# Encoder block on one core: every operation of the MLP in a fixed order per engine, by half products

## The chip, the cores and the metric

The kernel runs on one core of a Trainium2 chip. The metric is the device time of one execution in microseconds (us). The core's engines each work through their own instruction stream in order: TensorE (PE; its weight loads are listed as PEld), VectorE (DVE), ScalarE (ACT), GpSimd (POOL), and SyncE (SP), whose queue issues the large transfers. An instruction waits for work of other engines by semaphores. TensorE's results land in PSUM, which has eight banks of 128x512 float32 here; VectorE and ScalarE read them from there. All other tiles lie in SBUF.

## The reference

One layer: a mixer (2-D neighbourhood attention beside a gated linear attention), then an MLP, then a last norm. All is float32, 1024 tokens by 1024 columns, 4096 columns inside the MLP.

```python
def sqrelu_mlp(h, ln_g, w1, w2):
    u = rmsnorm(h, ln_g) @ w1
    return jnp.square(jax.nn.relu(u)) @ w2

def reference(...):
    h = x
    h = h + hybrid_mixer(h, ...)                # projections, two attentions, @ w_out
    h = h + sqrelu_mlp(h, ln_ff_g, w_ff1, w_ff2)
    return rmsnorm(h, ln_final_g)
```

## The kernel before

Everything is kept transposed: 128 columns on the partitions, 512 tokens (`H`) or all 1024 along the free dimension. A float32 product is made of three TensorE products with a reduced-precision type: each operand x is split into a high part (`h`, a cast on ScalarE) and a low part (`l = x - h`, a difference on VectorE or GpSimd, in `to_two`), and h·h, h·l and l·h are added in PSUM. So each 128x512 operand costs one cast and one difference, and each 128x128 by 128x512 block costs three matmuls.

The projections, the two attentions and `w_out` come first; they are the same program before and after. The residual sum lies in `hT`, the normalized MLP input of the first 512 tokens in `n0`. Then comes the MLP, in eight chunks of 512 of the 4096 inner columns. Chunk 0 is computed plainly (`FirstPlain` for w1, `SecondPlain` for w2, 16 half products each). Meanwhile the second 512 tokens are normalized (`normed_h`, from the factor `r1`), and the sums of the MLP input that the later chunks need are formed (`sums123`, `sum4`, helped by `whole`, which adds a high and a low part on GpSimd).

Chunks 1 to 7 use Winograd's form of Strassen's scheme: 2x2 blocks with seven products in place of eight, in `First` (w1) and `Second` (w2). The weight quarters A11 to A22 (512 KB each, four buffers, so that a new quarter's transfer waits until an older one has been read for the last time) are combined into S1 to S4, the inner activations B11 to B22 into T1 to T4. `KW` and `KB` say which pair makes which product 1 to 7. Each product is done as two half products of 12 matmuls (128x512). In `First` a half product g gives a bank of PSUM; ScalarE copies it (line 1028) or VectorE adds it to an earlier one (1031), and the squared ReLU is taken by ScalarE (1025, 1026) or in one VectorE instruction (1032). In `Second` a product's two halves i = 0, 1 accumulate in the same four banks j = 0 to 3, and after i = 1 VectorE adds the banks to `hT` (1078).

What sets the order: TensorE's matmuls, the transfers and ScalarE's casts keep the order in which the code issues them. `go_on` calls `prep_to`, which prepares two half products ahead (the sums that they need, casts and differences), then `mm` issues the 12 matmuls. All other VectorE and GpSimd operations are placed by the framework's scheduler by its own priorities. The sums S and T are all on GpSimd (959, 1047 to 1054; S as one 128x1024 operation), and of each pair of `Second`'s activation halves one difference `ul` is on GpSimd and one on VectorE (894).

After the last product but one, `square` and `finish` compute the final norm: squares on ScalarE, their sum over the columns on VectorE, one matmul with ones (`vf`), the factor `fy`, the products with `hT`, and the transfers out. The last product of the last chunk is done in two halves of 256 tokens, the first with its `square` and `finish` ahead of the second.

Of the kernel before, what the change touches and what calls it, by code (L numbers as in the profile page):

```python
# [63 lines left out]
def block_kernel(ctx, tc, xT, g_mix, w_in, w_z, rpb, na_mask, gu, gb, g_gla, sel_f, sel_b,  # L64
# [42 lines left out]
    class Ordered:  # L107


        def matmul(self, *args, **kw):  # L110
            tc.keep_in_program_order(nc.tensor.matmul(*args, **kw))  # L111
# [823 lines left out]

    yg_pool.close()
# [6 lines left out]
    KB = {1: "B11", 2: "B21", 3: "B22", 4: "T4", 5: "T1", 6: "T2", 7: "T3"}  # L943
    nchunk = FF // P // FCH
    HP = H

    class Quarters:


        def __init__(self, src, order=("A11", "A21", "A22", "A12")):  # L950
            self.t = {}
            for q in order:
                self.t[q] = mw.tile([P, D], F32, tag="raw", name=q, bufs=4)
                tc.keep_in_program_order(DMA.dma_start(self.t[q], src[("A11", "A12", "A21", "A22").index(q)]))

        def sum(self, dst, a, b, op, own=False):
            t = self.t
            o = mu.tile([P, D], F32, tag="S", name=dst) if own else t[own_of[dst]]
            G.tensor_tensor(o, t[a], t[b], op=op)  # L959
            t[dst] = o  # L960

        def need(self, key):
            if key in self.t:
                return
            if key == "S1":
                self.sum("S1", "A21", "A22", ALU.add, own=True)
            elif key in ("S2", "S3"):
                self.sum("S3", "A11", "A21", ALU.subtract)
                self.sum("S2", "A22", "S3", ALU.subtract)
            elif key == "S4":  # L970
                self.sum("S4", "A12", "S2", ALU.subtract, own=True)

        def parts(self, key, i):
            self.need(key)
            ph = mp.tile([P, HP], F32R, tag="ph", name="ph", bufs=3)
            pl = mp.tile([P, HP], F32R, tag="pl", name="pl", bufs=3)
            to_two(ph, pl, self.t[key][:, i * HP:(i + 1) * HP], kept=True)
            return ph, pl

    own_of = {"S3": "A21", "S2": "A11"}  # L980
# [4 lines left out]
    def uparts(x, eng):  # L985
        uh = mp.tile([P, H], F32R, tag="uh", name="uh", bufs=3)
        ul = mp.tile([P, H], F32R, tag="ul", name="ul", bufs=3)
        to_two(uh, ul, x, eng, kept=True)
        return uh, ul

    npt = {"B11": (n0, 0), "B21": (n0, 4)}
    first, last = lambda p: p in (1, 2, 5), lambda p: p in (4, 3, 2)

    class First:

        order = [(p, g) for p in (1, 5, 6, 3, 7, 2, 4) for g in range(2)]

        def __init__(self, c):
            self.w, self.u, self.b = Quarters(w1[c]), {}, {}
            self.sums = {}  # L1000

        def prep(self, p, i):
            r = self.w.parts(KW[p], i)
            if i:
                self.w.need({1: "S1", 5: "S2"}.get(p, KW[p]))
            return r

        def mm(self, p, g, w):
            if first(p):
                self.b[p in (1, 6, 7, 4), g] = bank("mm" if p == 1 else "s", f"u{p}_{g}")  # L1010
            o = self.b[p in (1, 6, 7, 4), g]
            t, k0 = npt[KB[p]]
            for k in range(4):
                for a, x in ((w[0], 0), (w[0], 1), (w[1], 0)):
                    PE.matmul(o, a[:, k * P:(k + 1) * P], t[:, k0 + k, x, :], start=first(p) and k == x == 0 and a is w[0],
                              stop=k == 3 and a is w[1], skip_group_check=True)
            self.evac(p, g, o)

        def evac(self, p, g, o):
            u = self.u  # L1020
            if p in (1, 5, 6, 4):
                k = {1: "B11", 5: "B22", 6: "B12", 4: "B21"}[p]
                u[k, g] = ub(f"u{k}{g}")
                if p == 4:
                    S.activation(u[k, g], o, AF.Relu)
                    S.activation(u[k, g], u[k, g], AF.Square)
                else:
                    S.copy(u[k, g], o)
            else:
                t = u[{2: "B11", 7: "B22", 3: "B12"}[p], g]  # L1030
                V.tensor_tensor(t, t, o, op=ALU.add)
                V.scalar_tensor_tensor(t, t, 0.0, t, op0=ALU.max, op1=ALU.mult)

    class Second:

        order = [(p, i) for p in (1, 5, 6, 3, 7, 2, 4) for i in range(2)]

        def __init__(self, c, u):
            self.w, self.u, self.b, self.c = Quarters(w2[c]), u, {}, c

        def prep(self, p, i):
            u, key = self.u, KB[p]
            if (key, i) not in u:
                b11, b12, b21, b22 = (u[k, i] for k in ("B11", "B12", "B21", "B22"))
                if key == "T1":
                    u[key, i] = ub("T1")
                    G.tensor_tensor(u[key, i], b12, b11, op=ALU.subtract)  # L1047
# [9 lines left out]
            if i:  # L1057
                self.w.need({1: "S1", 5: "S2"}.get(p, KW[p]))
# [291 lines left out]
```

## Time and profile before

| | us |
|---|---|
| median of 3 runs (lowest, highest) | 1307.57 (1305.16, 1313.53) |
| profiled execution, its time | 1304.25 |
| its span, first to last instruction | 1302.5 |
| TensorE busy in it | 1182.5 |
| VectorE busy | 959.1 |
| ScalarE busy | 597.9 |
| GpSimd busy | 494.5 |
| mean granted TensorE clock | 0.955 of full |

The span runs from the first to the last instruction; the execution's own time is 1.75 us longer. The MLP takes the part from 550 us to the end. A line of the timeline gives start, duration, engine, source line, operation, output and inputs, shapes, count, and in brackets the idle time before it with what ended it. Neighbouring instructions of a kind are merged (x2, x3). The matmul of 128x512 is listed at 0.39 us, but the next one starts 0.23 us after it; the start-to-start distance is what counts.

### The profile page before, as it was taken

The numbers are of one execution on the slowest core, as the hardware profiler recorded it, in microseconds if no ns is written. First come the engines' busy times: TensorE is split into PE (matmuls) and PEld (weight loads), VectorE is DVE, ScalarE is ACT, GpSimd is POOL, SyncE is SP. The second block draws the span as 40 slices with busy tenths as digits, with TensorE's granted clock in tenths as the row PEclk, the third lists the DMA queues.
The fourth block names the chain that finished last, engine by engine and source line by source line (L and its number), as shares of the span: only waits on it lengthen the run. The fifth ranks groups of instructions, "written<-read, shape, count | busy, mean of one in ns | idle before, by whom it ended". The sixth has DMA issues, their size and how long they took to land.

```text
span 1302.5 us, 15274 instructions
## 1 busy us (share of the span) xinstructions
PE 1182.5 (91%) x5530; PEld 956.4 (73%) x5530; DVE 959.1 (74%) x1500; ACT 597.9 (46%) x1129; POOL 494.5 (38%) x290
## 2 busy tenths in 40 slices
PE   9989999899999998967899898998989989989882
PEld 8867777678778787756678686786877868868661
DVE  8787877678687865757656867957669578686796
ACT  6667547456566654344323333333333333333373
POOL 4311011222313234314533637526456175362723
PEclk8999999899999999989899999998999999999895
DMA  7211000011111422201001110110111101111003
GB/s 218 71 51 35 30 33 33 18 53 45 34 45 41 166 77 85 97 1 65 33 33 65 49 49 33 65 65 33 50 49 65 49 33 51 63 49 49 32 1 129
DMA packets 37259, 73.01 MB, mean 56 GB/s; under 512 B 8928, under 2 KB 20320, under 8 KB 37184
## 3 DMA queue, kind: packets, MB, share of 16 engines
q1 hardware_dynamic: 36608, 71.11, 16.3%
q8 instruction: 43, 0.70, 0.2%
q0 software_dynamic: 432, 0.93, 0.2%
q14 instruction: 32, 0.26, 0.1%
q10 hardware_dynamic: 144, 0.00, 0.0%
HBM read 67.84 MB, written 5.96 MB: 57 GB/s over the span
## 4 chain that ended last, share of the span: by engine, by line
PE 53%; DVE 23%; POOL 12%; ACT 6%; issue 4%; DMA 1%; SPq 0%; DVEq 0%; POOLq 0%; ACTq 0%
PE u L111 18%; PE f L111 12%; PE proj L111 11%; PE op L111 6%; DVE pl L894 3%; POOL ul L894 2%; POOL uB L1051 2%; POOL T L1047 2%; POOL A L959 2%; PE sc L111 2%; POOL S L959 2%; DVE ul L894 1%; PE no L111 1%; POOL uB L1048 1%; DVE st L567 1%
## 5 line engine op out<-in xcount | busy, mean ns | idle before, releaser
L111 PE MATMUL f<-ul,ph 128*128 128x512 f32 (+1 forms) x464 | 191.2, 412 | 37.8 <-POOL ul L894 36.5
L172 POOL TENSOR_TENSOR wl<-wf,wh 128x1024 fp32r<-128x1024 f32 x36 | 89.4, 2484 | 334.1 <-ACT wh L171 314.1
L894 DVE TENSOR_TENSOR pl<-A,ph 128x512 fp32r<-128x512 f32 x164 | 167.0, 1028 | 59.8 <-ACT ph L891 58.9
L111 PE MATMUL f<-uh,ph 128*128 128x512 f32 (+1 forms) x464 | 188.9, 407 | 6.5 <-ACT uh L891 4.6
L111 PE MATMUL f<-uh,pl 128*128 128x512 f32 (+1 forms) x464 | 187.8, 405 | 0.2 <-DVE pl L894 0.2
L891 ACT CAST ph<-A 128x512 fp32r<-128x512 f32 x164 | 101.2, 620 | 183.1 <-PE f L111 92.9
L111 PE MATMUL proj<-nh,wh 128*128 128x512 f32 x352 | 150.8, 428 | 0.2 <-DVE qd L253 0.2
L111 PEld LDWEIGHTS f<-ul,ph 128*128 128x128 f32 x464 | 93.3, 201 | 65.7 <-POOL ul L894 43.3
L959 POOL TENSOR_TENSOR S<-A,A 128x1024 f32<-128x1024 f32 x28 | 70.7, 2527 | 181.6 <-DMA A<-in_w 166.3
L111 PE MATMUL proj<-nh,wl 128*128 128x512 f32 x352 | 139.6, 397 | 0.0
L111 PE MATMUL proj<-nl,wh 128*128 128x512 f32 x352 | 139.3, 396 | 0.0
L1078 DVE TENSOR_TENSOR hT<-hT,f 128x512 f32<-128x512 f32 (+1 forms) x200 | 122.3, 664 | 0.8 <-PE f L111 0.8
L111 PEld LDWEIGHTS f<-uh,ph 128*128 128x128 f32 x464 | 93.0, 200 | 29.9 <-ACT uh L891 7.8
L111 PEld LDWEIGHTS f<-uh,pl 128*128 128x128 f32 x464 | 93.3, 201 | 18.7 <-DVE pl L894 0.4
L111 PE MATMUL u<-n,ph 128*128 128x512 f32 x288 | 90.7, 397 | 13.1 <-ACT ph L891 13.1
L894 POOL TENSOR_TENSOR ul<-uB,uh 128x512 fp32r<-128x512 f32 x42 | 62.1, 1479 | 79.5 <-ACT uh L891 74.0
L959 POOL TENSOR_TENSOR A<-A,A 128x1024 f32<-128x1024 f32 x28 | 75.4, 2693 | 38.6 <-DVE pl L894 37.6
L894 DVE TENSOR_TENSOR pl<-S,ph 128x512 fp32r<-128x512 f32 x56 | 46.6, 841 | 54.8 <-ACT ph L891 54.3
L111 PEld LDWEIGHTS proj<-nh,wh 128*128 128x128 f32 x352 | 67.0, 190 | 19.2 <-issue 5.2
L111 PE MATMUL u<-T,ph 128*128 128x512 f32 x256 | 79.9, 394 | 0.8 <-ACT ph L891 0.8
L111 PEld LDWEIGHTS proj<-nh,wl 128*128 128x128 f32 x352 | 67.1, 191 | 15.2
L111 PE MATMUL op<-y,wh 128*128 128x512 f32 x240 | 77.0, 402 | 0.4 <-DVE y L663 0.4
(297 smaller groups left out, 2601.9 us busy)
## 6 DMA issues: line engine op xcount, KB each, us to landing
A<-in_w SPq DMA_DIRECT2D x64, 512.0 KB
wf<-in_w_in SPq DMA_DIRECT2D x22, 512.0 KB
wf<-in_w_out SPq DMA_DIRECT2D x17, 512.0 KB
hT<-in_xT SPq DMA_DIRECT2D x2, 2048.0 KB
xs<-in_xT SPq DMA_DIRECT2D x6, 512.0 KB
out<-hT SPq DMA_DIRECT2D x4, 512.0 KB
out<-hT SPq DMA_DIRECT2D x8, 256.0 KB
rpb<-rpb SPq DMA_DIRECT2D x16, 96.0 KB
```

The lines of the kernel that those rows point to most:

```text
L111: tc.keep_in_program_order(nc.tensor.matmul(*args, **kw))
L172: (eng or V).tensor_tensor(wl[:, c], wf[:, c], wh[:, c].bitcast(F32), op=ALU.subtract)
L567: V.scalar_tensor_tensor(st[64:128, j - 1, :], st[64:128, j, :], dec[64:128, j:j + 1], st[64:128, j - 1, :], op0=ALU.mult, op1=ALU.add)
L891: c = S.copy(h, x)
L894: (eng or V).tensor_tensor(l, x, h.bitcast(F32), op=ALU.subtract)
L959: G.tensor_tensor(o, t[a], t[b], op=op)
L1047: G.tensor_tensor(u[key, i], b12, b11, op=ALU.subtract)
L1048: G.tensor_tensor(b12, b22, b12, op=ALU.subtract)
L1051: G.tensor_tensor(b11, b11, u["T3", i], op=ALU.add)
L1078: V.tensor_tensor(hT[:, d, c], hT[:, d, c], o[:, s], op=ALU.add)
```

## The change

Only the MLP and the last norm are written anew. Now every operation of the MLP, on every engine, keeps the order in which the code issues it (`kp`), except for a few at the start and the last norm. The same matmuls are done, except for the order of products in `First` (1, 2, 6, 5, 3, 7, 4 in place of 1, 5, 6, 3, 7, 2, 4) and of the three matmuls per block in the second products (the one with `ul` is last, it was second).

- `prepare(k)` issues what is due while half product k runs: sums from PSUM of half k-1, early sums, differences for k+1 and k+2 and casts for k+2, late sums, and the activations of half k-1.
- All S and T sums move to VectorE, each as two 128x512 operations (`Weights.sum`, `tsum`). T1, T2, T3, T4 are formed by another chain of differences; T1 is formed within `First`, and S1 and S3 of the w2 weights too (`First.late`, p = 7 and 4).
- The squared ReLU is always two ScalarE operations (`relu2`); VectorE's is gone.
- In `Second` both activation differences `ul` of a pair are on GpSimd. They wait for a gate: the last matmul of bank j = 0 of an i = 1 half, the one after which VectorE adds bank 0 to `hT`. So they run while VectorE adds from PSUM. In `SecondPlain` both are on VectorE. GpSimd keeps `whole` (now 12 calls) and a part of the last products with `fy`.
- The sum matmul for `r1` comes after one half product (it was two), and the eight normalizations of the second token half are spread over half products 2 to 7, the sums over 8 to 23.
- At the end the last product's two token halves follow each other on TensorE with only the sum for tokens 512 to 1023 (`vf_10147`) between them; the other two sums come after. The factor `gfin` is applied in the same VectorE instruction as `fy`.

```diff
-        def sum(self, dst, a, b, op, own=False):
-            o = mu.tile([P, D], F32, tag="S", name=dst) if own else t[own_of[dst]]
-            G.tensor_tensor(o, t[a], t[b], op=op)
+        def sum(self, dst, i):
+            t, (place, a, b, op) = self.t, self.table[dst]
...
+            c = slice(i * H, (i + 1) * H)
+            kp(V.tensor_tensor(t[dst][:, c], t[a][:, c], t[b][:, c], op=op))
+    def relu2(u, x):
+        kp(S.activation(u, x, AF.Relu))
+        kp(S.activation(u, u, AF.Square))
...
+    class First(Stage):
+        def late(self, p, g):
+            for key in {1: ("S2",) if g else ("S3",), 2: ("S1",)}.get(p, ()):
...
+            if p == 6:
+                self.w.sum("S4", g)
+            if p == 7:
+                t = u["B12", g]
+                kp(V.tensor_tensor(t, t, u["B11", g], op=ALU.subtract))
+            if p == 4:
+                for i in range(2):
+                    self.after.w.sum("S3" if g else "S1", i)
...
+    class Second(Stage):
+        place = {"T1": "B12", "T2": "B12", "T3": "B11", "T4": "B21"}
+        def early(self, p, i):
+            for key, n in {(1, 0): (("S2", 0),), (1, 1): (("S4", 0),), (5, 0): (("T2", 0),),
...
+                (self.w.sum if key[0] == "S" else self.tsum)(key, n)
+        def prep2(self, p, i):
+            x = self.u[self.place.get(KB[p], KB[p]), i]
+            if i:
+                self.hu[p, i] = uhigh(x)
+                self.hw[p, i] = self.w.high(KW[p], i)
+            else:
+                self.pw[p, i] = self.w.low(self.w.high(KW[p], i))
+                self.hu[p, i] = uhigh(x)
+        def prep1(self, p, i):
+            if i:
+                self.pw[p, i] = self.w.low(self.hw[p, i])
+        def lows(self, p, i, gate=None):
+            self.pu[p, i], op = ulow(self.hu[p, i], G)
+            if gate is not None:
+                tc.add_manual_dep(op.ins, gate.ins.name,
...
-                for n, (a, x) in enumerate(((wh, uh), (wh, ul), (wl, uh))):
+                for n, (a, x) in enumerate(((wh, uh), (wl, uh), (wh, ul))):
...
                 if i:
-                    self.evac(p, j, o, s)
+                    self.add(p, j, o, s)
+                if j == 0:
+                    for st, q in lows:
+                        st.lows(*q, gate=m)
...
-    def prep_to(n):
-        while len(ready) < min(n, len(halves)):
-            st, p, i = halves[len(ready)]
-            ready.append(st.prep(p, i))
+    def prepare(k):
+        halves[k - 1][0].sums(*halves[k - 1][1:])
+        st.early(p, i)
+        for n, what in ((k + 1, "prep1"), (k + 2, "prep2")):
+                getattr(halves[n][0], what)(*halves[n][1:])
+        st.late(p, i)
+        halves[k - 1][0].acts(*halves[k - 1][1:])
+        for do, args in jobs.get(k, ()):
+            do(*args)
...
+    for n, k in enumerate((2, 3, 3, 4, 5, 5, 6, 7)):
+        job(k, normed, ("B12", "B22")[n // 4], n % 4)
...
-    for c0 in (0, Q):
-        for i in range(2):
-            f2.mm(4, i, ready[k + i], slice(c0, c0 + Q))
-        for d in range(NK):
-            square(c0, Q, d)
-        finish(c0, Q, (V, V, G, V))
+    for n in range(2):
+        for i in range(2):
+            f2.mm(4, i, s=s)
+        square(n * Q, Q, range(4, 8), n)
+        if n == 0:
+            finish(H, H, sumsq(H, H, fc["h1"]), 4)
+    for n in range(2):
+        finish(n * Q, Q, sumsq(n * Q, Q, fc["h0"][:, s], fc[n]), 2)
```

How the instructions stand at three places follows. A row gives the line, the operation, the output and its inputs. First GpSimd at the start of `Second` of chunk 7, before: S sums (`A`, `S`), T sums (`T`, `uB`) and the differences `ul`.

```order
L959 TENSOR_TENSOR A_9447<-A_9445,A_9447 128x1024
L894 TENSOR_TENSOR ul<-uB_9470,uh 128x512
L959 TENSOR_TENSOR A_9445<-A_9449,A_9447 128x1024
L1047 TENSOR_TENSOR T_9727<-uB_9549,uB_9470 128x512
L1048 TENSOR_TENSOR uB_9549<-uB_9510,uB_9549 128x512
L1051 TENSOR_TENSOR uB_9470<-uB_9470,uB_9549 128x512
L894 TENSOR_TENSOR ul<-T_9727,uh 128x512
```

And the same place on GpSimd after the change:

```order
L958 TENSOR_TENSOR ul<-uB_9524,uh 128x512
L958 TENSOR_TENSOR ul<-uB_9544,uh 128x512
L958 TENSOR_TENSOR ul<-uB_9605,uh 128x512
L958 TENSOR_TENSOR ul<-uB_9623,uh 128x512
L958 TENSOR_TENSOR ul<-uB_9605,uh 128x512
```

GpSimd has nothing left there but the differences of products 1, 5, 6 and so on, two for each product. Next VectorE at the same place, before; `pl` is the low part of a weight half, `hT<-hT,f` the add of a bank to `hT`:

```order
L894 TENSOR_TENSOR pl<-A_9445,ph 128x512
L894 TENSOR_TENSOR ul<-uB_9491,uh 128x512
L894 TENSOR_TENSOR pl<-S_9710,ph 128x512 x2
L1078 TENSOR_TENSOR hT<-hT,f_0_9738 128x512
L894 TENSOR_TENSOR ul<-T_9754,uh 128x512
L1078 TENSOR_TENSOR hT<-hT,f_1_9742 128x512
```

After the change, the last VectorE rows of `First` (S1 and S3 of the w2 weights) and the first of `Second`, up to the adds of product 1 and the T2 sum of product 5:

```order
L975 TENSOR_TENSOR S_9741<-A_9492,A_9494 128x512 x2
L975 TENSOR_TENSOR A_9492<-A_9490,A_9492 128x512 x2
L975 TENSOR_TENSOR A_9490<-A_9494,A_9492 128x512
L958 TENSOR_TENSOR pl<-A_9490,ph 128x512
L958 TENSOR_TENSOR pl<-S_9741,ph 128x512
L975 TENSOR_TENSOR A_9490<-A_9494,A_9492 128x512
L975 TENSOR_TENSOR S_9741<-A_9496,A_9490 128x512
L1140 TENSOR_TENSOR hT<-hT,f_0_9796 128x512
L1140 TENSOR_TENSOR hT<-hT,f_1_9800 128x512
L1140 TENSOR_TENSOR hT<-hT,f_2_9804 128x512
L1140 TENSOR_TENSOR hT<-hT,f_3_9808 128x512
L1087 TENSOR_TENSOR uB_9605<-uB_9642,uB_9605 128x512
```

The S and T sums stand between VectorE's differences and adds now, as single 128x512 operations, and no `ul` is left there. Last, VectorE in the closing norm, before, from the factor of tokens 512 to 1023 (`fu` to `fy`, 128x512) on:

```order
L206 SCALAR_TENSOR_TENSOR fy<-ft,fy 128x512
L1078 TENSOR_TENSOR hT<-hT,f_2_9746 128x256
L1249 TENSOR_TENSOR hT<-hT,fy 128x512 x2
L1078 TENSOR_TENSOR hT<-hT,f_3_9750 128x256
L1238 TENSOR_TENSOR fsq<-fsq 128x256 x7
L201 TENSOR_SCALAR fu<-vf_10130 128x256
```

And after:

```order
L208 SCALAR_TENSOR_TENSOR fy<-ft,fy 128x512
L203 TENSOR_SCALAR fu<-vf_10213 128x256
L1360 SCALAR_TENSOR_TENSOR hT<-hT,gfin,fy 128x512 x4
L1140 TENSOR_TENSOR hT<-hT,f_0_9796 128x256
L1140 TENSOR_TENSOR hT<-hT,f_1_9800 128x256
L1140 TENSOR_TENSOR hT<-hT,f_2_9804 128x256
L1140 TENSOR_TENSOR hT<-hT,f_3_9808 128x256
L1342 TENSOR_TENSOR fsq<-fsq 128x256 x3
```

Now four products with `fy` and the first factor of tokens 0 to 255 (`vf_10213`) stand ahead of the adds of the last 256 tokens, and three sums of squares follow in place of seven.

More of the change, by code (lines that the diff above doesn't have):

```diff
@@ L991, in block_kernel, with early, late, prep1 @@
+    def relu2(u, x):
+        kp(S.activation(u, x, AF.Relu))
+        kp(S.activation(u, u, AF.Square))
     npt = {"B11": (n0, 0), "B21": (n0, 4)}
[L992 to L1011 removed]
+    class Stage:
+        gated = False
+        def early(self, p, i): pass
+        def late(self, p, i): pass
+        def prep1(self, p, i): pass
+        def sums(self, p, i): pass
+        def acts(self, p, i): pass
+        def lows(self, p, i): pass
```

373 lines of the change are left out of this document (214 added, 159 removed).

## The prediction

> **What bounds the kernel now.** I read the page's busy times first, then the chain that ended last in order of time, then the timeline of TensorE. The page:
>
> ```profile
> PE 1182.5 (91%) x5530; PEld 956.4 (73%) x5530; DVE 959.1 (74%) x1500; ACT 597.9 (46%) x1129; POOL 494.5 (38%) x290
> ```
>
> TensorE is the busiest engine; what it does not do is wait. The change keeps its work, so it can win only TensorE's waits. The chain says where the stages begin (start, duration, engine, tile, line):
>
> ```profile
> 573.92 18.24 PE u L111 x72
> 673.08 29.93 PE u L111 x132
> 1180.16 29.97 PE u L111 x132
> ```
>
> `First` of chunk 1 starts at 673.08 and of chunk 7 at 1180.16, so a chunk takes (1180.16 − 673.08) / 6 = 84.51 us. The timeline of TensorE in one of these chunks:
>
> ```profile
> 842.56 0.39 PE L111 MATMUL u<-n,pl 128*128 128x512 f32 x1
> ...
> 879.96 0.39 PE L111 MATMUL u<-T,pl 128*128 128x512 f32 x1
> ...
> 885.40 0.39 PE L111 MATMUL f<-uh,pl 128*128 128x512 f32 x1
> 886.30 0.51 PE L111 MATMUL f<-uh,ph 128*128 128x512 f32 x1 [0.51 <-ACT uh L891]
> 889.89 0.79 PE L111 MATMUL f<-ul,ph 128*128 128x512 f32 x1 [3.08 <-POOL ul L894]
> 890.48 0.63 PE L111 MATMUL f<-uh,pl 128*128 128x512 f32 x1
> ...
> 894.32 0.63 PE L111 MATMUL f<-uh,pl 128*128 128x512 f32 x1
> ...
> 898.78 0.50 PE L111 MATMUL f<-ul,ph 128*128 128x512 f32 x1 [0.81 <-POOL ul L894]
> ```
>
> From the third matmul of `First` (842.56) to its last, the 168th (879.96), are 165 steps: 37.40 / 165 = 0.2267 us. `First` never waits. A chunk's 336 matmuls at that rate are 76.17 us, so 84.51 − 76.17 = 8.34 us per chunk are lost, all in `Second`: 3.1 us on `ul` from GpSimd, 1.3 in the two short waits, and then a slow run: from 890.48 to 894.32 are nine steps of 0.427 us. The windows show the granted clock (column behind the five busy times) for it and for full work:
>
> ```profile
> 890.00:894.70 4.70, 4.70 (x11) 3.69 (x12) 2.83 (x4) 1.80 (x4) 4.62 (x3) 0.50 0.00 0
> 900.00:910.00 10.00, 10.00 (x45) 8.27 (x45) 9.68 (x16) 3.89 (x7) 1.73 (x2) 1.00 0.07 20
> ```
>
> Twelve matmuls at half clock cost 12 × (0.427 − 0.227) = 2.4 us. And the chain names what TensorE waited for, a row of GpSimd work:
>
> ```profile
> 881.00 2.90 POOL A L959
> 883.90 1.70 POOL T L1047
> 885.67 1.27 POOL uB L1048
> 887.02 1.59 POOL uB L1051
> 888.61 1.23 POOL ul L894
> ```
>
> **The chunks, part by part.** The S and T sums leave GpSimd, so 7.4 of the 8.7 us of this row go. They become VectorE work; what a difference costs there, and GpSimd's `ul`, shows in the group by tile (nanoseconds: least, median, most):
>
> ```profile
> L894 POOL TENSOR_TENSOR ul<-uB,uh x42: 1280/1462/1779, 709.0 to 1261.6; 128x512 fp32r<-128x512 f32 x42
> L894 DVE TENSOR_TENSOR ul<-uB,uh x42: 676/687/2883, 711.9 to 1264.0; 128x512 fp32r<-128x512 f32 x42
> L1078 DVE TENSOR_TENSOR hT<-hT,f x200: 405/673/682, 718.3 to 1287.7; 128x512 f32<-128x512 f32 x96, 128x256 f32<-128x256 f32 x4
> 1254.30 2.47 DVE L1078 TENSOR_TENSOR hT<-hT,f 128x512 f32<-128x512 f32 x4
> 1254.45 1.30 POOL L1054 TENSOR_TENSOR uB<-uB,uB 128x512 f32<-128x512 f32 x1 [1.83 <-DVE ul L894]
> ```
>
> A difference of two SBUF tiles takes 0.69 us alone and up to 2.88 beside GpSimd. The add from PSUM never takes over 0.68, and at 1254 four of them ran beside a GpSimd sum, 2.47 us together, both unhindered. So the gate does what it is for, if it opens in time.
>
> VectorE in `Second` after the change: 14 `pl`, four S halves, six T halves, that is 24 × 0.69 = 16.6 us, and 28 adds, 7 × 2.47 = 17.3: 33.9 us against 14 × 12 × 0.2267 = 38.1 of TensorE. In `First`: 14 `pl`, 12 S halves, two T1, six sums from PSUM, 34 × 0.69 = 23.5 against 38.1. Squared ReLU moves six VectorE operations to twelve on ScalarE, which at the page's 46% has room. So VectorE fits, but tightly: a pair of halves in `Second` lasts 5.44 us, and the common load of four adds and four differences takes 5.23; the first pair has five differences. The closest deadline is `pl` of an i = 1 half, made in the half before: VectorE ends its adds some 0.9 us into that half (the last bank closes with the previous half; then latency and one add), does one sum and this `pl` by 2.3, and TensorE wants it as its second matmul at 2.72 + 0.23 = 2.95. That is 0.65 us of slack.
>
> The new wait: `ul` at its gate. Behind it in GpSimd's queue stands only the next `ul`; TensorE waits for both. Bank 0 closes 0.68 us into the half, with a latency of 0.4 the gate is open at 1.1, the first `ul` is done at 2.4, wanted as third matmul at 3.17; the second at 3.7, wanted at 5.9. Each has about 0.8 us or more to spare. Weights: S1 and S3 now need their quarters earlier.
>
> ```profile
> 654.41 3.39 DMA A<-in_w
> ```
>
> That is how long the chain waited for a quarter. A21 and A22 for `First` are issued some 1.5 us into the last half product but one, so they should land at 4.9; the S3 sum reads A21 at about 7. Nothing is due for that. I leave 1.0 us per chunk for short waits (bounds 0 and 4, the latter half of today's loss); such waits are too short to halve the clock. Today's loss from 673.08 to the last 512-wide matmul (58 us: six chunks at 8.34, and 7.7 in the seventh, below) becomes 7: **51 us won**.
>
> At the clock a rule is worth weighing. The Trainium skill (TensorE: Matmul & The Clock Gate, Part 1, "What's actually happening") says that TensorE falls to half clock after an idle window of about 3.4 us and comes back after about as much work. The half-clock stretch above, 4.7 us behind a 3.1 us wait, agrees roughly. By it the small leftover waits of chunk 0 (below) would cost no clock either, and the sum would come out 2 us lower.
>
> **Chunk 0.** TensorE and VectorE at its start:
>
> ```profile
> 550.36 0.73 PE L111 MATMUL u<-n,ph 128*128 128x512 f32 x2 [2.01 <-ACT ph L891]
> 561.68 2.08 DVE L886 SCALAR_TENSOR_TENSOR nf<-hT,gff,r 128x512 f32<-128x512 f32 x3
> 573.92 1.22 PE L111 MATMUL u<-n,ph 128*128 128x512 f32 x2 [11.11 <-ACT ph L891]
> ```
>
> Its 384 matmuls (87.0 us) and the sum for `r1` (0.5) take 122.7 us, from 550.36 to 673.08: 35.2 lost, 11.1 of them at 573.92, where the next weight's cast stood behind all eight normalizations. Now these are spread. `r1` comes one half product earlier, 2.7 us, near 559. A cast on ScalarE, from the groups by line (count, busy us, mean ns):
>
> ```profile
> L891 ACT CAST ph<-A 128x512 fp32r<-128x512 f32 x132 | 82.0, 622 | 171.6 <-PE f L111 88.4 <-PE u L111 83.1
> ```
>
> So each normalization now costs VectorE 0.69, a wait for its cast of 0.62, and 0.69 again: 2.0 us. Eight of them and six `pl` take 16 + 4 = 20 us, up to 579; TensorE wants the last of them at the end of half product 9, at 550.4 + 1 + 27 = 578. So a wait of 1 to 3 us is left there. In the next eight halves, a pair has eight VectorE operations, two waits for casts and a GpSimd `whole` beside them, 6.2 to 7.5 us against 5.44: 3 to 8 us behind, less the lead of some 4. With one spell of half clock the loss is 2 to 15 us; I take 7, nearer the low end since the later `SecondPlain` halves are light. **28 us won** (35.2 − 7).
>
> **The end.** TensorE and VectorE in the last stretch:
>
> ```profile
> 1258.21 0.39 PE L111 MATMUL f<-uh,pl 128*128 128x512 f32 x1
> 1268.70 8.80 POOL L1249 TENSOR_TENSOR hT<-hT,fy 128x512 f32<-128x512 f32 x6 [5.82 <-DVE fy L206]
> 1268.88 3.31 DVE L1249 TENSOR_TENSOR hT<-hT,fy 128x512 f32<-128x512 f32 x2
> 1272.44 6.94 DVE L1238 TENSOR_TENSOR fsq<-fsq 128x256 f32<-128x256 f32 x7
> 1279.43 1.22 PE L111 MATMUL vf<-fsq,ones 128*128 128x256 f32 x2 [11.55 <-DVE fsq L1238]
> 1294.95 3.15 DVE L1249 TENSOR_TENSOR hT<-hT,fy 128x256 f32<-128x256 f32 x6
> ```
>
> From the last 512-wide product (T = 1258.6) to the end (1302.5) are 43.9 us, 11.6 of them TensorE waiting in `vf` for VectorE's sums. After, that sum no longer stands between the token halves, so they end near T + 10. Then VectorE is the bound, in the order shown: the factor for tokens 512 to 1023 near T + 13, four products at 3.31 / 2 each beside GpSimd (T + 20), adds of the last 256 tokens and three sums (3 us), factor and six products (4), the last factor and six products (5), and what follows the last product today, 1302.5 − 1298.1 = 4.4: T + 36. If GpSimd hinders less, T + 28; if the pile of sums ahead is later, T + 41. I take 34.5: **9.4 us won**.
>
> **Sum.** 28.2 + 50.8 + 9.4 = 88.4. Against the profiled execution's own 1304.25 that is 1215.9. The median shown is 3.3 above this execution; I put 1217.
>
> **Rivals.**
> 1. The second `ul` spills over the adds. Two `ul` take 2 × 1.28 = 2.56 us against 2.47 of adds, so it ends just after them, beside VectorE's next sum. If that sum then stands still for a whole `ul`, a pair takes 5.23 + 1.28 = 6.5 against 5.44, and 49 pairs lose 1.1 each: 1217 + 52 − 7 = 1262. Against it: the spill is 0.1 to 0.5 us, and as matmul and adds wait for the same event a late TensorE brings them into step. Chance 0.10. The Trainium skill (SBUF — State Buffer, "Who interferes with whom") has this as a rule: an operation of VectorE with two SBUF inputs and a GpSimd one that reads SBUF lock each other out for the whole instruction, and one SBUF input is free of it. The adds at 1254 agree.
> 2. VectorE is tight without that: missed deadlines of half a us in most pairs, or quarters that land late: 3 to 5 us per chunk, 1240. Chance 0.15.
> 3. Slower: GpSimd and VectorE lose step for good. Both `ul` then fall beside differences: a pair is 5.23 + 2.56 = 7.8 us, a wait of 2.4 us each, with half clock behind it another 2.4, 49 pairs: 1217 + 235 − 7 = 1445. It starts where VectorE is over 0.65 us late in each pair and TensorE's wait does not let it catch up. That the gate hangs on the same matmul as the adds speaks against it. Chance 0.04.
> 4. No change: the clock gives way when the gaps go. At a mean of 0.87 the seven chunks' 533 us of matmuls take 533 / 0.87 = 613, and 1217 + 80 = 1297. The full clock through 900 to 910, with no gap, speaks against it. Chance 0.03.
>
> **How the numbers follow.** The forecast has 0.68. Its bounds: chunk 0 at 2, no loss in the chunks and the end at T + 28 give 1217 − 5 − 7 − 6.5 = 1198; 15, 4 per chunk and T + 41 give 1253. All ends at once are unlikely; with rival 2 inside and a step toward rival 1 the range is 1199 to 1255. A gain or loss of 1%, 13 us, is what a measurement here can tell from none. Faster takes all but rivals 3 and 4: 0.93; within 1% 0.03; slower 0.04.
>
> **What would show it.** Right: `Second` as even as `First`, a chunk near 77 us, GpSimd's `ul` at 1.28 us inside the adds, no half clock after 600 us, chunk 1 starting near 645, the 11.6 us wait in `vf` gone. Wrong: `pl` or `ul` named as what TensorE waits for in every pair (rivals 1 to 3), VectorE's sums over 1 us, a clock under 0.95 without gaps, or a chunk 0 that ends after 655.

## The result, and the profile after

The changed kernel takes 1218.57 us (median; 1217.17 to 1219.34) against 1306.52 us before (1305.16 to 1313.53): a ratio of 0.9316, 95% interval 0.9281 to 0.9351. The prediction said 1217. The sum came out right to 1.6 us, but not term by term. With the marks of the prediction (the profiled execution of after has a span of 1216.6 us):

| us | before | after | predicted | won |
|---|---|---|---|---|
| MLP's first matmul at | 550.36 | 548.99 | (unchanged) | 1.4 |
| chunk 0, to the start of `First` of chunk 1 | 122.7 | 101.0 | 94.5 | 21.7 |
| chunks, from there to the last 512-wide product T | 585.5 | 527.7 | 534.7 | 57.8 |
| T to the end | 43.9 | 38.9 | 34.5 | 5.0 |

The page's busy times, and the chain that ended last in the chunks (start, duration, engine, tile, line, count):

```profile
PE 1152.3 (95%) x5534; PEld 940.2 (77%) x5534; DVE 923.4 (76%) x1582; ACT 643.3 (53%) x1193; POOL 299.9 (25%) x209
```

```profile
649.99 38.08 PE u L111 x168
688.07 38.08 PE f L111 x168
...
1145.03 19.73 PE f L111 x87
```

Where before every `Second` took 46.4 us, every stage is now 38.08 = 168 × 0.2267: TensorE does not wait once in the chunks. The windows of chunk 0's two stages (`FirstPlain`, `SecondPlain`), and of a `First` and a `Second` (width, then busy us and count of PE, PEld, DVE, ACT, POOL, then the granted clock, the DMA share and GB/s):

```profile
549.00:597.10 48.10, 46.65 (x194) 35.78 (x194) 35.37 (x54) 28.59 (x51) 3.08 (x2) 1.00 0.12 44
597.10:649.80 52.70, 47.31 (x192) 36.85 (x193) 40.99 (x55) 19.53 (x35) 13.21 (x8) 0.97 0.12 41
```

```profile
649.83:687.91 38.08, 38.08 (x170) 31.53 (x169) 23.63 (x35) 21.20 (x37) 2.90 (x2) 1.00 0.16 56
687.91:725.99 38.08, 38.08 (x170) 31.53 (x169) 33.22 (x54) 16.27 (x28) 15.31 (x12) 1.00 0.16 56
```

`Second` keeps VectorE busy for 33.2 of 38.1 us (the prediction counted 33.9). One pair of halves there, from the timelines of VectorE and GpSimd (start, duration, what; in brackets the idle time before it and what ended it):

```profile
696.95 2.73 DVE L1140 TENSOR_TENSOR hT<-hT,f 128x512 f32<-128x512 f32 x4 [0.30 <-PE f L111]
699.59 0.69 DVE L975 TENSOR_TENSOR S<-A,A 128x512 f32<-128x512 f32 x1
```

```profile
697.05 2.55 POOL L958 TENSOR_TENSOR ul<-uB,uh 128x512 fp32r<-128x512 f32 x2 [2.89 <-PE f L111]
```

Both `ul` end at 699.60, with the four adds (699.68), and the next VectorE sum takes 0.69 us, unhindered.

Chunk 0 is uneven. From the timelines of VectorE, GpSimd and TensorE in `SecondPlain`, and the windows of the last stretch:

```profile
603.63 3.47 DVE L958 TENSOR_TENSOR ul<-u,uh 128x512 fp32r<-128x512 f32 x2
607.03 0.68 DVE L1306 TENSOR_TENSOR b<-b 128x512 f32<-128x512 f32 x1
608.39 0.69 DVE L958 TENSOR_TENSOR T<-b,T 128x512 fp32r<-128x512 f32 x1 [0.69 <-ACT T L1271]
```

```profile
603.25 1.61 POOL L1267 TENSOR_TENSOR b<-n 128x512 f32<-128x512 f32 x1 [12.82 <-issue]
604.82 1.74 POOL L1267 TENSOR_TENSOR b<-nt 128x512 f32<-128x512 f32 x1
```

```profile
629.05 0.47 PE L111 MATMUL f<-uh,ph 128*128 128x512 f32 x1 [1.99 <-DVE hT L1196]
```

```profile
628.00:632.00 4.00, 2.94 (x8) 2.42 (x9) 4.00 (x8) 1.67 (x4) 0.00 (x0) 0.71 0.00 0
```

The two sums h + l on GpSimd (L1267) lie beside VectorE's two `ul`, which take 3.47 us instead of 1.3; then VectorE waits 0.69 us for a cast. A pair of halves lasts 607.03 to 613.01, 5.98 us, where TensorE needs 5.44; TensorE ends up waiting 1.99 us for the sums from PSUM, and half clock follows.

The end, from the timelines of VectorE, GpSimd and TensorE:

```profile
1176.23 4.29 DVE L1342 TENSOR_TENSOR fsq<-fsq 128x512 f32<-128x512 f32 x3
1193.31 6.57 DVE L1360 SCALAR_TENSOR_TENSOR hT<-hT,gfin,fy 128x512 f32<-128x512 f32 x4
1199.80 1.40 DVE L1140 TENSOR_TENSOR hT<-hT,f 128x256 f32<-128x256 f32 x4
```

```profile
1175.77 3.39 POOL L958 TENSOR_TENSOR ul<-uB,uh 128x512 fp32r<-128x512 f32 x2 [2.44 <-PE f L111]
```

```profile
1183.56 0.58 PE L111 MATMUL f<-uh,pl 128*128 128x256 f32 x1 [4.34 <-DVE pl L958]
1202.65 1.22 PE L111 MATMUL vf<-fsq,ones 128*128 128x256 f32 x2 [9.80 <-DVE fsq L1342]
```

Three sums of squares stand ahead of the last adds and the last `pl`, which costs TensorE 4.34 us. They stand where the gated pair of `ul` should meet adds from PSUM, and take 4.29 us beside that pair. Four output products stand ahead of the last 256 tokens' adds, and the wait in `vf` is 9.80 us, where it was 11.55.

### The profile page after: what moved, and what is told of

The parts are those of the page before. It is cut to its first block, busy times and chain, and to the rows that moved or that the text cites. A ratio compares the mean times of both kernels' runs of the same rounds, so it can differ in the third digit from the quotient of the medians.

```text
span 1216.6 us, 15294 instructions
## 1 busy us (share of the span) xinstructions
PE 1152.3 (95%) x5534; PEld 940.2 (77%) x5534; DVE 923.4 (76%) x1582; ACT 643.3 (53%) x1193; POOL 299.9 (25%) x209
## 4 chain that ended last, share of the span: by engine, by line
PE 70%; DVE 19%; ACT 6%; issue 3%; POOL 1%; DMA 1%; DVEq 0%; SPq 0%; ACTq 0%; POOLq 0%
PE f L111 23%; PE u L111 22%; PE proj L111 12%; PE op L111 6%; DVE st L569 2%; PE sc L111 2%; PE no L111 2%; DVE nl L284 1%; PE pt L116 1%; DVE st L566 1%; DVE pl L958 1%; DVE hT L1360 1%; PE o L111 1%; DVE ul L958 1%; DVE b L492 1%
## 5 line engine op out<-in xcount | busy, mean ns | idle before, releaser
L958 POOL TENSOR_TENSOR ul<-uB,uh 128x512 fp32r<-128x512 f32 x98 | 128.7, 1332 | 426.0 <-ACT uh L993 289.9
L980 ACT CAST ph<-A 128x512 fp32r<-128x512 f32 x176 | 109.2, 621 | 158.6 <-PE f L111 77.1
L111 PE MATMUL f<-uh,ph 128*128 128x512 f32 (+1 forms) x464 | 181.5, 391 | 4.9 <-DVE hT L1196 3.4
L111 PE MATMUL f<-uh,pl 128*128 128x512 f32 (+1 forms) x464 | 180.5, 389 | 4.3 <-DVE pl L958 4.3
L111 PE MATMUL f<-ul,ph 128*128 128x512 f32 (+1 forms) x464 | 180.8, 390 | 0.7 <-DVE ul L958 0.5
L958 DVE TENSOR_TENSOR pl<-A,ph 128x512 fp32r<-128x512 f32 x176 | 119.0, 686 | 58.8 <-ACT ph L980 58.8
L1140 DVE TENSOR_TENSOR hT<-hT,f 128x512 f32<-128x512 f32 (+1 forms) x200 | 131.7, 675 | 21.5 <-PE f L111 21.5
L993 ACT CAST uh<-uB 128x512 fp32r<-128x512 f32 x98 | 60.5, 618 | 56.7 <-PE f L111 37.8
L111 PEld LDWEIGHTS proj<-nl,wh 128*128 128x128 f32 x352 | 66.8, 190 | 11.4 <-issue 1.4
L111 PE MATMUL u<-nt,ph 128*128 128x512 f32 x224 | 69.0, 389 | 0.0
```

The source lines that it names most:

```text
L111: m = nc.tensor.matmul(*args, **kw)
L958: return kp(eng.tensor_tensor(l, x, h.bitcast(F32), op=ALU.subtract))
L980: kp(S.copy(ph, x))
L993: kp(S.copy(uh, x))
L1140: kp(V.tensor_tensor(hT[:, d, c], hT[:, d, c], o[:, s], op=ALU.add))
```

## The experiments

All start from the changed kernel. The kernel before ran beside them with medians of 1303.5 to 1305.5, so a difference of 2 or 3 us between medians is read together with the stages' lengths in the trace. A `Second` is worked out as the distance from one `First` to the next in the chain, less 38.08.

### The wait of `ul` at its gate

```diff
-            if gate is not None:
+            if False:
```

> The two GpSimd differences of a pair no longer wait for the first bank of the half before; nothing else is moved. Theory (the wait is what keeps them beside VectorE's sums from PSUM): each ul now starts as soon as its rounded half is cast, some 4.8 us earlier by the idle time GpSimd shows before a pair, and falls on VectorE operations with two SBUF inputs, which pay about the length of one ul for each pair (1.3 us or more). Seven pairs make 9 us per Second, on a VectorE that has 38.1 - 33.2 = 4.9 us to spare in a Second: Seconds of 40 to 43 us instead of 38.08 and, with the clock, 1235 to 1265 us. Rival (any order of the ul is good enough, the gain came from taking the S and T sums off GpSimd): every stage stays within 0.5 us of 38.08, 1216 to 1222 us.

Measured: 1247.01 us (1246.01 to 1247.94), 28.4 more. The chain, then VectorE, GpSimd and TensorE in one `Second`, and its window:

```profile
648.92 38.09 PE u L111 x168
...
729.06 38.09 PE u L111 x168
```

```profile
701.54 1.77 DVE L958 TENSOR_TENSOR pl<-A,ph 128x512 fp32r<-128x512 f32 x1
```

```profile
700.98 3.48 POOL L958 TENSOR_TENSOR ul<-uB,uh 128x512 fp32r<-128x512 f32 x2 [0.26 <-ACT uh L993]
```

```profile
703.37 0.50 PE L111 MATMUL f<-uh,pl 128*128 128x512 f32 x1 [1.24 <-DVE pl L958]
```

```profile
686.90:728.90 42.00, 38.97 (x170) 31.25 (x169) 39.19 (x53) 16.09 (x28) 18.44 (x12) 1.00 0.16 51
```

`Second` is 42.05 us, `First` still 38.08. An `ul` that starts when its cast is done falls on differences, which grow from 0.69 to as much as 1.77 us. VectorE's work grows by 6.0 us per `Second`, and TensorE waits for `pl`, not for the `ul` that came early. The theory holds, with a time in the middle of its range.

```diff
-                if j == 0:
+                if j == 1:
                     for st, q in lows:
```

> The same wait, hung on the second bank of the half before instead of the first: both ul of a pair start 0.68 us later. The first then ends about 3.1 us into the half, beside a wanted time near 3.17; the second ends near 4.4 us, some 0.7 to 0.9 us behind the end of the four sums from PSUM, beside VectorE's next difference. Theory (a spill costs VectorE what overlaps, and VectorE has 4.9 us to spare in a Second): the next difference grows from 0.68 to 1.3 or 1.6 us, 4 to 6 us per Second, which the slack takes nearly whole: Seconds of 38.1 to 39.0 us, 1218 to 1228 us. Rival of the prediction (a spill blocks VectorE's next difference for a whole ul): 9 us per Second, Seconds of 41 to 43 us, above 1240 us. Rival that the first ul comes late instead: TensorE waits behind ul in each pair, 0.1 to 0.5 us, and the clock with it, 1225 to 1250 us.

Measured: 1218.62 us, no change. The window of a `Second`, and one pair:

```profile
687.40:725.60 38.20, 38.20 (x170) 31.38 (x169) 35.91 (x53) 16.20 (x28) 15.31 (x12) 1.00 0.17 56
```

```profile
699.08 1.25 DVE L975 TENSOR_TENSOR S<-A,A 128x512 f32<-128x512 f32 x1
```

```profile
697.22 2.55 POOL L958 TENSOR_TENSOR ul<-uB,uh 128x512 fp32r<-128x512 f32 x2 [2.95 <-PE f L111]
```

The difference behind the adds takes 1.25 us instead of 0.69. That is 2.7 us of VectorE per `Second` (35.91 against 33.22), and TensorE pays 0.13 us of it. So rival 1 of the prediction has a real mechanism with a wrong price: the overlap from 699.08 to 699.77 costs 0.56 us, not a whole `ul`, and there is slack for it. The first `ul` was not late either: TensorE waited for an `ul` once in the seven chunks, 0.5 us.

### The sums on GpSimd, and the order

First S alone, then S and T, both at their places in the fixed order:

```diff
-            kp(V.tensor_tensor(t[dst][:, c], t[a][:, c], t[b][:, c], op=op))
+            kp(G.tensor_tensor(t[dst][:, c], t[a][:, c], t[b][:, c], op=op))
```

> The sums of the weights (S1 to S4, as halves, at the same places of the order) go back from VectorE to GpSimd; the gated ul and all else stay. VectorE loses 8 operations of 0.68 us per stage, GpSimd gains 8 of 1.3 us or more, which run beside VectorE operations with two SBUF inputs and stand in GpSimd's row ahead of the gated ul. Theory (the sums in GpSimd's row were the loss of the chunks before): an S sum that begins beside VectorE's work delays the pl that reads it and the ul behind it; 2 to 6 us per chunk plus half clock, 1235 to 1265 us. Rival (only the sum of VectorE's work counts, and taking 5.4 us per stage off it can only help): stages at 38.08 us, 1215 to 1219 us.

```diff
-            kp(V.tensor_tensor(u[pl[key], i], u[pl.get(a, a), i], u[pl.get(b, b), i], op=ALU.subtract))
+            kp(G.tensor_tensor(u[pl[key], i], u[pl.get(a, a), i], u[pl.get(b, b), i], op=ALU.subtract))
```

> The sums of the weights (S1 to S4) and those of the tokens' half products (T2 to T4) both stand on GpSimd, as halves at the places of the fixed order; the gated ul stay. With the S sums alone there it cost 3.0 us (1221.57 against 1218.57). Theory 1 (sums in GpSimd's row are harmless where their places are chosen): six T sums more per Second, 1.3 to 1.8 us each, each ahead of a cast and an ul with about 2 us to spare; 0.5 to 2 us per Second, 1221 to 1235 us. Theory 2 (as the prediction had it: sums in GpSimd's row are the loss of the chunks before, whatever their place): TensorE waits for ul in several products of each Second, 3 to 6 us per chunk with the clock, 1240 to 1260 us.

Then the order given up (TensorE's matmuls keep theirs), with the engines of the changed kernel, and with S and T on GpSimd:

```diff
-    kp = tc.keep_in_program_order
+    kp = lambda i: i
```

> The MLP's instructions of VectorE, ScalarE, GpSimd and the weight loads are no longer held in the order of the program; the scheduler places them by its own measures, as in the kernel before. Engines, tiles and the wait of the ul stay. Theory (the fixed order carries a part of its own): differences wanted within half a microsecond stand behind sums wanted later; waits for pl and ul of 1 to 4 us per chunk and half clock return, 1230 to 1265 us. Rival (the gain is which engine does what, and the order only notes it): stages within 0.5 us of 38.08, 1216 to 1224 us.

> As the run with S and T sums on GpSimd, but the MLP's instructions are placed by the scheduler and not held in the order of the program; the wait of the ul stays. Free order alone cost 4.8 us (1223.38), S sums on GpSimd alone 3.0. Theory 1 (row and order act together: a long sum ahead of a wanted ul is what cost before, and the scheduler puts it there): more than the sum of the two, waits of TensorE behind ul of 1 us and more in several products, 1240 to 1285 us. Rival (they add up, and the wait of the ul is the one large part): about 1218.6 + 4.8 + the cost of the run in fixed order, 1225 to 1240 us.

Measured: S alone 1221.57, S and T 1230.60, free order 1223.38, S and T in free order 1246.95 us. From the chains of three of them, in this order (S and T; free order; both), the start of `First` of chunk 1 and of a later one, one chunk on or, in free order, two:

```profile
650.37 37.87 PE u L111 x167
...
728.18 37.87 PE u L111 x167
```

```profile
638.32 38.08 PE u L111 x168
...
795.52 38.08 PE u L111 x168
```

```profile
640.83 38.08 PE u L111 x168
...
723.84 38.08 PE u L111 x168
```

A mean `Second` (over three chunks; for the free order two) is 38.8 us with S on GpSimd, 39.7 with S and T, 40.5 in free order and 43.5 with both, beside 38.08 and, before, 46.4. S alone missed its theory and came out 2.6 us above the rival's 1215 to 1219, S and T lies inside theory 1's range. So the row of sums that the prediction read as the loss of the chunks costs only 1.6 of 8.3 us where each half sum has a chosen place and the gate stands; in the scheduler's order it costs 3.0 (43.5 − 40.5). Row and order act together: the time of the last of the four lies in its theory's range, and TensorE then waits for `ul` again, though in one long wait per `Second` and not in several products (what waited for what: us in total, times, longest):

```profile
PE f L111 <- POOL ul L958: 21.3, 6, 3.6
```

The largest single part is the gate, 4.0 us per `Second`; next the order, 2.4. Each of these is the price of giving one thing up in the changed kernel; what each would win in the kernel before, no run shows. They don't add up to 8.3 exactly, and what is left between 43.5 and 46.4 (one `ul` per pair on VectorE and no gate, whole S sums, another order of products and matmuls, VectorE's squared ReLU) wasn't tried by itself.

What the order does to a `Second` shows on GpSimd and VectorE in free order:

```profile
764.96 3.14 POOL L958 TENSOR_TENSOR ul<-uB,uh 128x512 fp32r<-128x512 f32 x2 [3.88 <-PE f L111]
```

```profile
765.15 1.78 DVE L975 TENSOR_TENSOR S<-A,A 128x512 f32<-128x512 f32 x1
```

The gated pair starts at the same matmul as ever, but the scheduler has put an S sum there, ahead of the adds, and it takes 1.78 us. The T sums take 1.21 us in the mean of the chunks (0.69 in the written order), and TensorE waits for `pl` 20 times, 10.2 us in all. So the order does part of the gate's work: it puts the adds where the gated `ul` run. That this is the whole of the 2.4 us isn't shown.

The free order's total lies where its rival put it, 1216 to 1224, but not for the rival's reason: its `Second` are 2.4 us longer, within the 1 to 4 us per chunk of the theory, and something else is shorter. TensorE's first matmul of the MLP:

```profile
545.33 0.61 PE L111 MATMUL u<-n,ph 128*128 128x512 f32 x2
```

Chunk 0, to 638.32, takes 93.0 us there, 8.0 less than in the written order, and it begins 3.7 earlier. The written order won 17.6 us in the chunks (527.7 against 545.3) and gave 13.4 back: 3.7 ahead of the MLP, 8.0 in chunk 0, 1.7 behind T.

### Chunk 0

```diff
         kp(S.copy(h, x))
-        low(l, x, h, V)
+        later.append((l, x, h))
...
+        put_lows()
         put(key, k, t)
...
-            whole(x[:, 0:H], "B21", k)
-            whole(x[:, H:D], "T2", k)
+            whole(x[:, 0:H], "B21", k, V)
+            whole(x[:, H:D], "T2", k, V)
```

> Chunk 0 alone is changed: VectorE issues the next normalization ahead of the difference of the one before (no VectorE operation waits any more for the cast of its own block), the same for the T1, T2 and T3 sums, and the two sums h + l for T4 stand on VectorE instead of GpSimd, so that they no longer lie beside VectorE's ul. Theory (chunk 0 lost 13.5 us of TensorE by VectorE's serial waits of 0.57 us behind each cast and by GpSimd beside two ul, which makes a pair of products 5.98 us instead of 5.44): the wait before the normalizations end, the three 6 us pairs come down to 5.44 us, and the wait for the first sums of Second at 623 us goes: 4 to 8 us less, 1210 to 1215 us. Rival (TensorE waits in chunk 0 are those of the start: the squares and the root at 549 to 557 us, the first T and B blocks): within 1.5 us of 1218.6.

Measured: 1221.40 us, 2.8 more; chunk 0 is 104.7 us. Both theories missed. The chain:

```profile
571.92 0.62 ACT B L1273
572.54 0.53 ACT ph L980
573.09 0.04 DVE pl L958
573.13 0.57 issue
573.70 0.76 DVE b L1288
```

The wait is of the same size as before, one instruction further: VectorE's `pl` now stands where the difference stood, and its own cast stands behind the block's cast on ScalarE. Besides, the sums for T4 were spread into the halves with VectorE's eight adds, and TensorE waited 3.0 and 2.0 us for those.

```diff
+        late = later[:]
+        del later[:]
         for do, args in jobs.get(k, ()):
             do(*args)
+        if getattr(halves[0][0], "held", None):
+            halves[0][0].low2()
+        lows_of(late)
...
-            job(8 + 2 * n + step, sums123, k, step)
+            job(8 + 2 * n + step if k else 15 + 2 * step, sums123, k, step)
...
-            job(16 + 2 * k + step, sum4, k, step)
+            job((18, 24, 26, 28)[k] + step, sum4, k, step)
```

> Chunk 0 alone is changed against the changed kernel, after a first try that only put off the differences made it 2.8 us longer: there pl stood behind a normalization whose cast stood ahead of pl's own cast on ScalarE. Now VectorE's row in each half product is normalization, pl (its cast asked for earlier), and last the difference of the half before; the sums h + l for T4 stand on VectorE, away from the halves with VectorE's eight sums from PSUM, and the last T1 to T3 sums are spread over three halves more. Theory (VectorE's row in chunk 0 is bound by waits for casts and by GpSimd beside it): the 0.57 us waits go, the pairs of products keep 5.44 us, the wait behind the sums from PSUM at 623 us shrinks; chunk 0 loses 6 to 10 us instead of 13.5: 1212 to 1216 us. Rival (VectorE has no time left in chunk 0 however it is ordered: 5.3 us of work in 5.44 per pair): within 2 us of 1218.6.

Measured: 1205.01 us (1204.31 to 1205.52), 13.6 less. Chunk 0 goes from 548.51 to 637.66, 89.1 us, where 384 matmuls and the sum need 87.5. `low2` is `pl`, whose cast is asked for ahead of the jobs; `late` holds the differences of the half before. Of the loss of 13.5 us that is 11.9, more than the theory had hoped, and the rival (no time left on VectorE) falls: VectorE had the time and spent it waiting. Which share is the waits and which GpSimd beside `ul` was not measured apart. In this run the low part of T3 is taken behind the sum that goes on with its block, so the small third product with T3 is of the wrong block and the output is not right; the instructions are the same. The run of "Both" below puts that difference in its place, and its chunk 0 takes 89.1 us too.

### The end

```diff
-    for n, ks in ((9, (0, 1)), (10, (2, 3, 4)), (11, (5, 6, 7))):
+    for n, ks in ((9, (0, 1)), (10, (2, 3, 4))):
...
+    prepare(len(halves) - 1)
+    square(H, H, (5, 6, 7), "h1")
...
+    rh = rms(H, vh)
+    square(Q, Q, range(4, 8), 1)
+    products(H, H, rh, 4)
```

> The end alone is changed, in order only: the last four half sums of squares stand behind the sums of product 2 and the last pl, and VectorE's output products of the second token half stand behind the last sums from PSUM and the sums of squares of the quarters. Theory (VectorE's row is what sets the end: T to the end is 38.9 us, with 4.34 us of TensorE waiting for the last pl and 9.80 us for the last sum of squares behind 6.57 us of products): pl is done at about T + 1.2 us, the quarters' sums by T + 13, 4 products of 6.6 us, then 6 and 6 of 3.4 us with 1.3 and 0.8 us for the two roots, and 4.3 us of the last transfer: T to end 30 to 33 us, 1210 to 1213 us. Rival (the products or the transfers bound the end, the order only moves the wait): within 1.5 us of 1218.6.

Measured: 1214.55 us, 4.0 less; T to the end is 35.7 us, not 30 to 33. Then the same order with all products on VectorE:

```diff
-    products(H, H, rh, 4)
+    products(H, H, rh, 0)
...
-        products(n * Q, Q, rms(Q, v), 2)
+        products(n * Q, Q, rms(Q, v), 0)
```

> The end in the new order (1214.55 us before this step), and GpSimd and ScalarE take no output products any more: VectorE does all 8 of each token part. Theory (GpSimd's products cost VectorE as much as they take off it, since both read two SBUF tensors: beside GpSimd's 5.59 us of products, four sums of squares of a quarter took 4.63 us instead of some 1.4, and four products 3.73 us): these sums come down by 3 us, eight products of 0.69 us take 5.5 us instead of 3.7, the quarters' eight of 0.42 us about 3.4 as six did; 1 to 3 us less, 1211.5 to 1213.5 us. Rival (taking a third of the products off VectorE is a gain whatever lies beside it): 3 to 5 us more, 1217 to 1220 us.

Measured: 1211.62 us, 2.9 less again, as the theory had it; T to the end is 33.5 us, 2.2 less. VectorE and GpSimd in the first of the two, VectorE in the second:

```profile
1191.21 4.63 DVE L1342 TENSOR_TENSOR fsq<-fsq 128x256 f32<-128x256 f32 x4
1195.77 3.73 DVE L1362 SCALAR_TENSOR_TENSOR hT<-hT,gfin,fy 128x512 f32<-128x512 f32 x4
```

```profile
1191.37 5.59 POOL L1365 TENSOR_TENSOR hT<-hT,fy 128x512 f32<-128x512 f32 x4 [11.38 <-DVE fy L208]
```

```profile
1190.43 1.81 DVE L1342 TENSOR_TENSOR fsq<-fsq 128x256 f32<-128x256 f32 x4
1192.16 5.38 DVE L1362 SCALAR_TENSOR_TENSOR hT<-hT,gfin,fy 128x512 f32<-128x512 f32 x8
```

The order shortens TensorE's waits (1.38 us for the last `pl`, 2.84 and 2.79 for the sums of squares) but moves GpSimd's products onto other VectorE work: 4.63 + 3.73 = 8.36 us beside GpSimd, 1.81 + 5.38 = 7.19 for the same sums and twice the products without it. GpSimd's help was worth less than nothing there.

```diff
-            if name in fc:
-                kp(V.tensor_tensor(fc[name], fc[name], sq, op=ALU.add))
+            if name == "h1" and name in fc:
+                kp(V.tensor_tensor(fc[name][0], fc[name][0], sq, op=ALU.add))
             else:
-                fc[name] = sq
+                fc.setdefault(name, []).append(sq)
```

> As the end on VectorE, and TensorE, which idles at the end, also adds up the squares of the last token half: four squares of the first product's half and four of each quarter go straight into the product with the ones, and nine VectorE sums (three of 0.68 us, six of about 0.36) go. Theory (VectorE's row sets the end, item after item): 4 us less than the end on VectorE, about 1208 us; TensorE pays sixteen matmuls of 256 columns of about 0.48 us each, 7.7 us, mostly beside VectorE's eight products. Rival (TensorE's added matmuls or the output transfers become the end): 1211 us or more.

Measured: 1209.42 us, 2.2 less by the medians. T to the end goes from 33.5 to 29.8 us, 3.7 of the expected 4; in the profiled execution the MLP began 0.8 us later.

### Both

The order of chunk 0 and the end with TensorE's sums, together. The one line that is new to chunk 0 takes the low part of T3 ahead of the sum that goes on with its block:

```diff
+            lows_of(late3)
             kp(V.tensor_tensor(b22, b22, b["B11", k], op=ALU.add))
```

> The order of chunk 0 (1205.01 us) and the end with TensorE's sums of squares (1209.42 us) together. In the run on chunk 0 alone the low part of T3 was taken behind the sum that goes on with its block, so its small third product was of the wrong block, with the same instructions; here that difference stands ahead of the sum. Theory (the two places are apart in time and their gains add up): 1218.57 - 13.56 - 9.15 = 1195.9 us, 1194 to 1198 us, ratio to the kernel before 0.916 to 0.919; the stages of the chunks stay at 38.08 us. Rival (the difference that moved up waits for its cast, four times 0.6 us, or the end's start is no longer the same): 1198 to 1202 us.

Measured: 1197.44 us (1197.26 to 1199.64), a ratio to the kernel before of 0.9183, 95% interval 0.9167 to 0.9198. That beats both kernels. The gains add up within 1.6 us, as its theory had it. Its stages of chunk 0:

```profile
548.80:593.70 44.90, 44.82 (x194) 36.45 (x195) 37.34 (x57) 31.52 (x56) 2.90 (x2) 1.00 0.14 47
593.70:637.90 44.20, 43.70 (x193) 35.86 (x192) 35.47 (x58) 17.61 (x32) 0.00 (x0) 1.00 0.14 48
```

## Why the prediction was right, and where it wasn't

**The chunks: 50.8 forecast, 57.8 measured.** The loss left was put at 7 us ("I leave 1.0 us per chunk for short waits"), and it is 0.0. The counts behind it hold: VectorE 33.2 us (33.9 counted), `ul` at 1.28 us each inside the adds, no deadline missed. That goes for six of the seven pairs. The first has no adds to lie beside: it runs without a gate in the last half of `First`, where two S sums take 3.49 us with it, and `First` has room for that. Of the 8.34 us lost per chunk before, the prediction named 6.8 (3.1 + 1.3 + 2.4), but it used the whole, which rests on the chain. And the reason given was only part: in the changed kernel the row of GpSimd sums is worth 1.6 us per chunk, the gate 4.0 and the order 2.4. An argument from the row alone would have forecast the same gain without the gate, and been 28 us wrong.

**Chunk 0: 28.2 forecast, 21.7 measured.** The loss was put at 7 and is 13.5, inside the bounds of 2 to 15. The step that failed is "nearer the low end since the later `SecondPlain` halves are light". `SecondPlain` takes 52.7 us for 43.5 us of matmuls, 9.2 of the 13.5, and nearly all of it falls in its first ten halves, up to 633 us. The last six are light, as said, and run without a wait; the first ten were given no loss of their own. The sums h + l for T4 beside VectorE's `ul` and the waits for casts, both counted for `FirstPlain`, weren't counted there.

**The end: 9.4 forecast, 5.0 measured.** The working came to T + 36, and 34.5 was taken; it is T + 38.9. The three sums of squares ahead of the last adds, seen as a possible "pile of sums", made it late, and so did the four products ahead of the last 256 tokens' adds, which took 6.57 us, as worked out: with both moved behind it is T + 35.7, and the share of each was not measured apart. The mark "the 11.6 us wait in `vf` gone" was wrong: 9.80 us are left, because the wait only moved from one token half to the next.

**The marks.** Chunk 1 starts at 649.99, not "near 645"; "no half clock after 600" fails at 629 and at 1184. At 629 this weighs the rule on the clock, too: by the Trainium skill (TensorE: Matmul & The Clock Gate, Part 1, "What's actually happening") chunk 0's short waits would cost no clock, as it takes an idle window of about 3.4 us. The trace disagrees: a granted clock of 0.71 from 628 to 632 behind a wait of 1.99 us, with one of 1.38 us five us earlier. The three waits of 0.8 to 1.2 us per `Second` without the gate left it at 1.00.

**The rivals.** Rival 1 (a spill blocks a difference for a whole `ul`): the next bank's gate shows 0.56 us per spill and 0.13 per `Second`, not 1.1 per pair. Rival 3 (engines out of step, 4.8 us per pair): without any gate it is 4.0 us per `Second`. VectorE's work grows there by 6.0 us and not by 2.56 per pair, against a slack of 4.9. Rivals 2 and 4 did not occur.

So the total was right to 1.6 us by luck in the terms: one that was 7 us too pessimistic stood against two that were 6.5 and 4.4 too optimistic, and the first matmul came 1.4 earlier.

## What to carry to other kernels

Where two engines hinder each other, say which work may overlap, and tie it there with a wait: here giving up the wait cost more (4.0 us per `Second`) than giving the slower engine its sums back (1.6). An order written by hand should be held against the scheduler's stage by stage, since it can win in the steady loop and lose at the start and the end. And help from a second engine is to be priced with what it does to the first: eight products on VectorE alone were quicker than four and four.

## What was not expected of the hardware

In the free order, GpSimd and VectorE in chunk 0, from their timelines:

```profile
566.38 17.96 POOL L1267 TENSOR_TENSOR b<-n 128x512 f32<-128x512 f32 x2 [25.92 <-DVE b L1282]
```

```profile
566.82 0.69 DVE L1291 TENSOR_TENSOR b<-b,b 128x512 f32<-128x512 f32 x1
...
581.27 0.68 DVE L958 TENSOR_TENSOR pl<-A,ph 128x512 fp32r<-128x512 f32 x1
583.13 1.75 DVE L1294 TENSOR_TENSOR b<-b,b 128x512 f32<-128x512 f32 x1 [1.18 <-POOL b L1267]
```

Two GpSimd sums that take 1.3 to 1.7 us each elsewhere last 17.96 us together, while VectorE issues one two-input operation after another, each at 0.69 us. The first ends 1.2 us after VectorE has nothing left but to wait for it, at 581.9. The Trainium skill (SBUF — State Buffer, "Who interferes with whom") says that the one that issues first has the shared pair for its whole instruction and the other blocks. The trace goes further: one GpSimd operation was kept out through 15 us of VectorE operations, though those from 566.82 on began after it. Without the gate it was let in, and VectorE's grew to 1.77 us instead; why it went the one way here and the other there, these runs don't show.
